# Decay logits and four keys' convolutions among the first products, and N stored whole, in a decoder step on one core

## The chip, the cores and the metric

The kernel runs on one core of a Trainium2 chip. Its engines are TensorE (PE), VectorE (DVE), ScalarE (ACT), GpSimd (POOL) and SyncE (SP). They run side by side and wait for each other through semaphores. SP and POOL issue most of the DMAs. The metric is the device time of one execution in microseconds, as the median of several runs. A profiled execution gives the trace.

## The reference, cut to what matters

One decoder layer for 512 prompt tokens and 8 sample tokens, D = 2048. A projection `w_in` gives q, k and v of 8 heads (128 wide), a gate z, a beta and a decay logit per head, and pool channels.

```python
qkv_c, new_conv = short_conv(conv_buf, qkv, conv_w)      # 4 taps along the tokens, then silu
q, k = l2norm(q) * (DN_HEAD_DIM ** -0.5), l2norm(k)
beta = jax.nn.sigmoid(b_raw)
g = -jnp.exp(a_log) * jax.nn.softplus(a_raw + dt_bias)
o, S = gated_delta_chunked(q, k, v, g, beta, S0)
dn_out = rmsnorm(o, dn_norm) * silu(z)
h = h + concat([dn_out, pool_out]) @ w_out
h = h + swiglu(rmsnorm(h, norm_ffn))
...
```

The gated delta rule needs, for each chunk of tokens, a triangular matrix N of k's inner products (weighted with beta and the decays), the inverse of 1 + N, here called U, and a state S that runs through the chunks.

## The kernel before

All activations lie transposed, channels on partitions and the 520 tokens (8 sample, 512 prompt) along the row. Each fp32 operand is split into a high and a low part, and a product takes three passes (high by high, low by high, high by low). ACT makes the high parts, DVE the low ones (`hi`, `lo`; `L294`/`L295` in pairs, `L135`/`L137` in plain products).

**Stages.** First x is turned and normed and the first two columns of `w_in` are multiplied (to some 48 us). Then come five pairs of columns: two plain ones (`Pair.plain`, called with `to_plain` and `to_strassen`) with tiles 10 to 13, which are keys 2 to 5, and three in Strassen's form (`strassen` with seven products of 24 matmuls each; the hook `after(q, j)` is called ahead of product j of pair q). In these two stages the order of every engine's instructions is the order of the program. From about 155 us on the woven stage follows: TensorE still goes in program order, the other engines in an order that a scheduler plans from priorities and estimated times; `tc.high_priority(offset=AHEAD)` lifts an instruction ahead of others. It computes the remaining columns with `product`, and between its steps `weave.step()` runs two tracks of generators: each `yield n` says that the next part comes n steps later. A tile of columns has 16 steps, and a step lies behind six matmuls. After the weave come `w_out` and the feed-forward part, up to the end at 2196 us, which the change doesn't touch.

**In the weave.** Track 0 starts with `states` (five pieces of sample states are transposed on TensorE at steps 11 to 15), later the recurrence `delta(h)`, one head after the other. Track 1 starts with `gates`: 64 products of `wba` with x for beta and decay logits (`L912`, `L913`), their transposes, some 35 small operations on DVE and ACT, and the sums of decays. Behind it come `keys(h)` for 8 heads: products of the convolved key with itself (`L1155`), its transposes (`L1158`), norms (ACT squares, POOL power), N (`L1170`) and kd (`L1172`); five steps later the diagonal 32 x 32 blocks of N are stored to `nd_d` and zeroed in N. N and k of heads 4 to 7 go to `kept_d`; all four share one place for N. Each `keys(h)` also convolves key h + 2 (`take_k`). `eliminate` loads the blocks (`nb`), inverts them in 31 steps of two DVE operations (`L1200`, `L1202`), stores U and its transpose to `ud_d`, loads them back as `utf` and adds `delta(0)` to the track, 60 steps later.

`delta(h)` first multiplies N by U (`L1234`), improves U in three iterations (`L1253`) and then goes through four chunks: R from S (`L1282`, `L1284`), W (`L1289`, ACT copy `L1291`), S (`L1294`, DVE `L1297` for the first chunk, `L1299` for others) and the output (`L1300`, `L1301`). `take_qv(h + 1)` convolves the next head's q and v in one go. A convolution (`convolved`) loads a column from `c_d`, and takes one DVE tensor-scalar (`L1097`), three taps of scalar-tensor-tensor (`L1099`) and a Silu on ACT (`L1100`).

PSUM has eight banks: three rotate as `mm` (products of the weave and of `product`), five as `dn` (all the rest). A tile takes the next bank in turn and waits until all reads of the bank's last tile are done.

## Time and profile before

| | |
|---|---|
| median of 3 runs | 2198.32 us (2196.6 to 2199.14) |
| the profiled execution | 2198.01 us |
| its span, first to last instruction | 2196.3 us |
| PE, DVE, ACT, POOL busy | 2139.0, 1786.2, 958.0, 455.7 us |
| mean granted TensorE clock | 0.994 |

A row of a view names the line of the kernel, the engine, the operation and its tiles as out<-in; times are microseconds from the start of the span. What stands in brackets behind a row is the engine's idle time before it and what ended it. Busy TensorE is not TensorE at its peak, since the ends of matmuls are modelled. A granted clock of 1.0 is 2.4 GHz, 0.5 is 1.2 GHz.

### The profile page before, as it was taken

The page shows a single profiled execution, that of the slowest core. Times are in us where ns is not written, and L with a number is a line of the kernel's source. Part 1 is how long each engine was busy: PE and PEld are TensorE (multiplying, and loading weights), DVE is VectorE, ACT ScalarE, POOL GpSimd, SP SyncE. Part 2 cuts the span into 40 slices and gives each one's busy share as a digit, 9 for nine tenths or more (in the row PEclk, how much of TensorE's full clock was granted, in tenths as well). Part 3 has the DMA queues.
Part 4 walks back from the last instruction along what each step waited for, and adds up shares of the span by engine and source line. Part 5 has one row for each costly group of instructions (what it writes and reads, how often), then busy time and mean ns, then how long its engine had stood idle before and what let it go on. Part 6 is the DMA issues. An engine that isn't in the chain of part 4 may idle for free.

```text
span 2196.3 us, 43075 instructions
## 1 busy us (share of the span) xinstructions
PE 2139.0 (97%) x17737; PEld 2127.6 (97%) x17737; DVE 1786.2 (81%) x2635; ACT 958.0 (44%) x1454; POOL 455.7 (21%) x559
## 2 busy tenths in 40 slices
PE   7999979999999999999999999999999999999998
PEld 7999979999999999999999999999999999999998
DVE  7788766665569979988888898888887798887997
ACT  6346513433335445343443443443433534435544
POOL 2112201110002210433323323323012402103100
PEclk9999989999999999999999999999999999999999
DMA  8444634432435552554555545445445836447333
GB/s 277 125 135 140 188 107 137 119 108 65 125 99 159 157 150 71 169 154 132 161 152 150 149 147 164 144 144 159 126 124 172 274 108 179 138 109 238 96 107 117
DMA packets 451553, 316.98 MB, mean 144 GB/s; under 512 B 27676, under 2 KB 424373, under 8 KB 448013
## 3 DMA queue, kind: packets, MB, share of 16 engines
q1 hardware_dynamic: 429741, 232.59, 37.5%
q0 software_dynamic: 20448, 80.91, 11.3%
q8 instruction: 139, 2.28, 0.4%
q10 hardware_dynamic: 1168, 0.74, 0.1%
q14 instruction: 57, 0.47, 0.1%
HBM read 261.97 MB, written 52.87 MB: 143 GB/s over the span
## 4 chain that ended last, share of the span: by engine, by line
PE 77%; DVE 11%; DMA 4%; ACT 3%; issue 3%; POOL 1%; SPq 0%; ACTq 0%; DVEq 0%; POOLq 0%
PE dn L301 21%; PE dn L302 21%; PE dn L303 21%; PE mm L170 3%; PE mm L172 3%; PE mm L171 3%; DVE lo L295 2%; DVE lo L137 1%; DMA vT<-c_d 1%; DVE y L1099 1%; ACT hi L294 1%; DVE raw L323 1%; DMA st<-a_d 1%; DMA raw<-in_w_in_dram 0%; DVE tm L1200 0%
## 5 line engine op out<-in xcount | busy, mean ns | idle before, releaser
L294 ACT CAST hi<-raw 128x1024 fp32r<-128x1024 f32 (+1 forms) x447 | 453.1, 1027 | 439.1 <-DVE raw L323 218.2
L295 DVE TENSOR_TENSOR lo<-raw,hi 128x1024 fp32r<-128x1024 f32 (+1 forms) x447 | 556.8, 1265 | 104.4 <-ACT hi L294 102.8
L170 PE MATMUL mm<-xh,hi 128*128 128x264 f32 (+1 forms) x960 | 291.1, 303 | 1.4 <-DVE ext L261 0.7
L171 PE MATMUL mm<-xl,hi 128*128 128x264 f32 (+1 forms) x960 | 272.5, 284 | 1.3 <-DVE xl L586 1.1
L172 PE MATMUL mm<-xh,lo 128*128 128x264 f32 (+1 forms) x960 | 272.6, 284 | 1.1 <-DVE lo L137 1.1
L170 PEld LDWEIGHTS mm<-xh,hi 128*128 128x128 f32 x960 | 182.7, 190 | 2.4 <-DVE ext L261 0.9
L171 PEld LDWEIGHTS mm<-xl,hi 128*128 128x128 f32 x960 | 183.0, 191 | 1.9 <-DVE xl L586 1.9
L172 PEld LDWEIGHTS mm<-xh,lo 128*128 128x128 f32 x960 | 181.9, 189 | 1.6 <-DVE lo L137 1.6
L323 DVE TENSOR_TENSOR raw<-raw 128x1024 f32<-128x1024 f32 (+1 forms) x136 | 180.5, 1327 | 2.3
L302 PE MATMUL dn<-b21l,hi 128*128 128x260 f32 x620 | 175.7, 283 | 0.1
L303 PE MATMUL dn<-b21h,lo 128*128 128x260 f32 x620 | 175.4, 283 | 0.0
L303 PE MATMUL dn<-b11h,lo 128*128 128x260 f32 x612 | 173.2, 283 | 1.8 <-DVE lo L295 1.8
L301 PE MATMUL dn<-b21h,hi 128*128 128x260 f32 x620 | 175.0, 282 | 0.0
L302 PE MATMUL dn<-b11l,hi 128*128 128x260 f32 x612 | 173.3, 283 | 0.0
L301 PE MATMUL dn<-b11h,hi 128*128 128x260 f32 x612 | 172.8, 282 | 0.0
L301 PE MATMUL dn<-T1h,hi 128*128 128x260 f32 x556 | 158.1, 284 | 0.0
L302 PE MATMUL dn<-T1l,hi 128*128 128x260 f32 x556 | 157.7, 284 | 0.0
L303 PE MATMUL dn<-T1h,lo 128*128 128x260 f32 x556 | 156.8, 282 | 0.0
L301 PE MATMUL dn<-B22h,hi 128*128 128x260 f32 x548 | 155.9, 284 | 0.0
L302 PE MATMUL dn<-B22l,hi 128*128 128x260 f32 x548 | 155.6, 284 | 0.0
L303 PE MATMUL dn<-B22h,lo 128*128 128x260 f32 x548 | 154.6, 282 | 0.4 <-DVE lo L295 0.4
L1605 POOL TENSOR_TENSOR mixa<-mixa 128x520 f32<-128x520 f32 x22 | 51.2, 2326 | 495.7 <-DVE mixa L1599 495.7
(729 smaller groups left out, 6923.2 us busy)
## 6 DMA issues: line engine op xcount, KB each, us to landing
raw<-in_w_gate_up_dram SPq DMA_DIRECT2D x134, 512.0 KB
raw<-in_w_in_dram SPq DMA_DIRECT2D x75, 512.0 KB
a_d<-mixa POOLq DMA_DIRECT2D x22, 1040.0 KB, 5.5
raw<-in_w_down_dram SPq DMA_DIRECT2D x48, 448.0 KB
mixb<-in_w_gate_up_dram SPq DMA_DIRECT2D x41, 512.0 KB
raw<-in_w_out_dram SPq DMA_DIRECT2D x25, 512.0 KB
st<-a_d POOLq DMA_DIRECT2D x49, 260.0 KB, 6.5
raw<-in_w_down_dram SPq DMA_DIRECT2D x24, 512.0 KB
```

The lines of the kernel that those rows point to most:

```text
L137: dve.tensor_tensor(lo[:, r], raw[:, r], hi[:, r].bitcast(F32), op=ALU.subtract)
L170: te.matmul(acc[ci], wh, hi[k][:, c0:c1], start=(i == 0), stop=False)
L171: te.matmul(acc[ci], wh, lo[k][:, c0:c1], start=False, stop=False)
L172: te.matmul(acc[ci], wl, hi[k][:, c0:c1], start=False, stop=(i == len(w) - 1))
L294: act.copy(hi, raw)
L295: dve.tensor_tensor(lo, raw, hi.bitcast(F32), op=ALU.subtract)
L301: te.matmul(acc, wh[:, k, :], xf[:, k, :], start=start and k == 0, stop=False)
L302: te.matmul(acc, wh[:, k, :], xg[:, k, :], start=False, stop=False)
L303: te.matmul(acc, wl[:, k, :], xf[:, k, :], start=False, stop=stop and k == wh.shape[1] - 1)
L323: dve.tensor_tensor(r[name], r[a], r[b], op=op)
L1099: dve.scalar_tensor_tensor(y, x[:, i:i + SEQ], cw(i, t), y, op0=ALU.mult, op1=ALU.add)
L1605: pool.tensor_tensor(q[:, 4:8:2, :], q[:, 1:4:2, :], q[:, 0:2, :], op=ALU.subtract)
```

## The change

The logits with all that follows from them (`gates`) become nine steps called from `to_plain` and `to_strassen`, with banks of the `mm` rotation and scratch in parts of `mixa`; the second half of the logit products stands ahead of the first pair, the first half in it. Their results move to another pool of tiles. Keys 2 to 5 are convolved between the Strassen products: loads at `after(0, 1)` and `after(1, 1)`, one operation per listed slot. In every convolution the load goes to POOL's queue, and the first tap from DVE to ACT. `keys` run in the order 2, 3, 0, 1, 4, 5, 6, 7, with 8 steps from one to the next up to the fifth and 11 from there on; only keys 0, 1 (ahead of the weave), 6 and 7 are convolved in the weave. N is stored whole to `nn_d` with one DMA on POOL, without zeroing; its blocks are loaded from there, those of heads 0 to 3 already after key 1. The blocks are zeroed later (`no_blocks`). `delta(0)` comes 58 instead of 60 steps after the elimination is issued. In `delta` the ten operations of the next q and v are spread, one per step, from the second iteration on; R, W and S get high priority.

```diff
+    def convolution(x, t, place):
+
+        ys = []
+
+        def load():
+            pool.memset(x[:, 0:3], 0.0)
+            pool.dma_start(x[:, 3:3 + SEQ], c_d[t])
+
+        def first():
+            ys.append(place())
+            act.activation(ys[0], x[:, 0:SEQ], AF.Copy, scale=cw(0, t))
+
+        def tap(i):
+            return lambda: dve.scalar_tensor_tensor(ys[0], x[:, i:i + SEQ], cw(i, t), ys[0], op0=ALU.mult, op1=ALU.add)
+
+        return [load, first, tap(1), tap(2), tap(3), lambda: act.activation(x[:, 3:3 + SEQ], ys[0], AF.Silu)]
...
             if i == 14:
+                split(wba[:, :, 0:16], wba[:, :, 16:32], wba_raw)
...
+        def row(k, a, b):
+            return mixa[:, k, HALF + a:HALF + b]
...
+        banks = {}
+
+        def bank(n):
+            banks[n] = ps_mm.tile([P, HALF], F32, tag="mm", name="mm")
+            return banks[n]
+
+        def logits(half):
+            pa, c = bank(f"a{half}")[:32, :], slice(HALF * half, HALF * half + HALF)
+            for k in range(KT):
+                te.matmul(pa, wba[:, k, :], xh[:, k, c], start=(k == 0), stop=False)
+                te.matmul(pa, wba[:, k, :], xl[:, k, c], start=False, stop=(k == KT - 1))
+
+        def logits_out(half):
+            c = slice(HALF * half, HALF * half + HALF)
+            dve.tensor_tensor(bas[:, c], banks[f"a{half}"][:32, :], rb[:32, c], op=ALU.mult)
...
+        def gates(step):
+            if step == 0:
+                logits(0)
+                logits_out(0)
+                act.activation(al, al, AF.Exp)
+            elif step == 1:
+                pt = bank("t")
+                for c in range(NCH):
+                    te.transpose(pt[:, 32 * c:32 * c + 32], bas[:, NB + P * c:NB + P * (c + 1)], ident[:32, :32])
+                te.transpose(pt[:NB, 128:160], bas[:, 0:NB], ident[:32, :32])
+            elif step == 2:
...
+                act.activation(u, ax, AF.Abs)
+                act.activation(u, u, AF.Exp, scale=-1.0)
+                act.activation(eb, eb, AF.Exp, scale=-1.0)
+            elif step == 3:
+                dve.tensor_scalar(s, u, 2.0, None, op0=ALU.add)
+                dve.reciprocal(s2, s)
...
+                dve.reciprocal(btok, eb)
+            elif step == 4:
+                pass
+            elif step == 5:
+                g4 = gtok[:, 0:4, :].rearrange("p c h -> p (c h)")
+                pg = bank("g")
+                te.matmul(pg[:, 0:32], triu, g4, start=True, stop=True)
+                te.matmul(pg[:, 32:64], stril, g4, start=True, stop=True)
+                te.matmul(pg[:, 64:96], ones, g4, start=True, stop=True)
+                for i in range(2):
+                    pr = bank(f"r{i}")
+                    for c in range(2):
+                        te.matmul(pr[:H, P * c:P * (c + 1)], gtok[:, 2 * i + c, :], triu, start=True, stop=True)
...
+            elif step == 6:
+                pg = banks["g"]
...
+            elif step == 8:
+                te.matmul(bank("e")[:, 0:128], ones[:NB, :], ds_.rearrange("p a b -> p (a b)"), start=True, stop=True)
+            else:
+                dve.tensor_copy(sgb.rearrange("p a h b -> p (a h b)"), banks["e"][:, 0:128])
         pairs = [InPair(14), InPair(24), InPair(26)]
+        logits(1)
         plain_pairs[0].cut("A12")
...
+        logits_out(1)
 
         def to_plain(step):
+            gates(step)
...
         def to_strassen(step):
+            gates(5 + step)
...
+        early = [convolution(places(h)[0], 8 + h, lambda k=k: mixa[:, 6 + k % 2, 0:SEQ]) for k, h in enumerate((2, 3, 4, 5))]
+        slots = [(0, 5), (0, 6), (1, 0), (1, 1), (1, 2), (1, 4), (1, 5), (1, 6), (2, 0), (2, 1), (2, 3), (2, 5), (2, 6)]
+
         def after(q, j):
 
+            if j == 1 and q < 2:
+                for c in early[2 * q:2 * q + 2]:
+                    c[0]()
+            if (q, j) == (0, 3):
+                early[0][1]()
+            if (q, j) in slots:
+                k, i = divmod(slots.index((q, j)), 3)
+                if i == 0 and k:
+                    early[k - 1][5]()
+                if k < 4:
+                    early[k][2 + i]()
+                if i == 1 and k < 3:
+                    early[k + 1][1]()
...
-        nd_d = dram.tile([H, 4, NCH, 32, 32], F32, name="nd_d")
-        ud_d = dram.tile([H, 4, 2, NCH, 32, 32], F32, name="ud_d")
+        nn_d = dram.tile([P, H * NCH, 4, 32], F32, name="nn_d")
+        ud_d = dram.tile([4, H, 2, NCH, 32, 32], F32, name="ud_d")
+        kept_d = dram.tile([4, 2, P, SEQ], F32, name="kept_d")
...
         def take_qv(h):
+
             x = [d1tile(tag, [P, 528], name)[:, 13:528] for tag, name in (("s0", "qT"), ("s2", "vT"))]
-            qvs[h] = convolved(x[0], h), convolved(x[1], 16 + h)
+            qvs[h] = [a[:, 3:3 + SEQ] for a in x]
+            q, v = (convolution(a, t, lambda: d1tile("y", [P, SEQ], "y")) for a, t in zip(x, (h, 16 + h)))
+            return [lambda: (q[0](), v[0]()), *q[1:5], lambda: (q[5](), v[1]()), *v[2:]]
...
+        def no_blocks(h):
+
+            nn3 = v3(mixb[:, 4 + h % 4, 0:SEQ])
+            for q in range(4):
+                r = slice(32 * q, 32 * q + 32)
+                pool.memset(nn3[r, :, r], 0.0)
...
-            if h + 2 < H:
-                take_k(h + 2)
+            if h in (0, 5):
+                take_k({0: 6, 5: 7}[h])
...
-            nn3 = v3(nn)
-            for q in range(4):
-                r = slice(32 * q, 32 * q + 32)
-                sp.dma_start(nd_d[h, q].rearrange("c s j -> s c j"), nn3[r, :, r])
-            for q in range(4):
-                r = slice(32 * q, 32 * q + 32)
-                pool.memset(nn3[r, :, r], 0.0)
+            pool.dma_start(nn_d[:, NCH * h:NCH * h + NCH], nn.rearrange("p (n r j) -> p n r j", n=NCH, r=4))
             if h >= 4:
-                for i, y in enumerate((kT, nn, kd)):
+                for i, y in enumerate((kT, kd)):
                     sp.dma_start(kept_d[h - 4, i], y)
             if h == H - 1:
                 weave.add(eliminate(), 1)
+            else:
+                if h == 1:
+                    nbs.append(d1tile("nb", [P, 32, 32], "nb"))
+                    blocks(0)
+                yield 3 if h < 4 else 6
+
+        nbs = []
+
+        def blocks(half):
+
+            for q in range(4):
+                p0 = 32 * q + 16 * half
+                pool.dma_start(nbs[0][p0:p0 + 16], nn_d.rearrange("(q s) n r j -> q r n s j", q=4)[q, q, 16 * half:16 * half + 16])
...
+            nb = nbs[0]
+            blocks(1)
+            for h in range(4):
+                no_blocks(h)
...
-            take_qv(0)
-            weave.add(delta(0), 0, 60)
+            for f in take_qv(0):
+                f()
+            weave.add(delta(0), 0, 58)
...
-            if h not in qvs:
-                while 16 + h not in traced:
-                    yield 1
-                take_qv(h)
-                yield 12
             qT, vT = qvs[h]
+            to_come = []
+
+            def more():
+                if to_come:
+                    to_come.pop(0)()
...
-                if it == 2 and 17 + h in traced:
-                    take_qv(h + 1)
+                    if h + 1 < H:
+                        assert 17 + h in traced
+                        to_come = take_qv(h + 1)
+                more()
...
+                    R = d1tile("R", [P, P], "R")
+                    with tc.high_priority(offset=AHEAD):
+                        dve.scalar_tensor_tensor(R, kp[:, 0:P], negc[:, c, h:h + 1], vs[:, ck(c)],
+                                                 op0=ALU.mult, op1=ALU.add)
+                    more()
...
-                act.copy(W, wp[:, 0:P])
+                with tc.high_priority(offset=AHEAD):
+                    act.copy(W, wp[:, 0:P])
+                more()
                 yield 2
...
+                with tc.high_priority(offset=AHEAD):
+                    if S is None:
+                        dve.tensor_copy(S2, dp[:, 0:P])
+                    else:
+                        dve.scalar_tensor_tensor(S2, S, egl[:, c, h:h + 1], dp[:, 0:P], op0=ALU.mult, op1=ALU.add)
...
+            if 0 < h < 5:
+                no_blocks(h + 3)
...
-        weave.add(gates(), 1)
-        for h in range(H):
+        for h in (2, 3, 0, 1, 4, 5, 6, 7):
             weave.add(keys(h), 1)
```

## Rows read from the trace of the kernel before

**Rows 1.** The page's first part: busy time, share of the span and instructions of each engine.

```profile
PE 2139.0 (97%) x17737; PEld 2127.6 (97%) x17737; DVE 1786.2 (81%) x2635; ACT 958.0 (44%) x1454; POOL 455.7 (21%) x559
```

**Rows 2.** Waits of TensorE in the window from 155 to 550 us: line, what it waited for: total, times, longest.

```profile
PE dn L1234 <- DMA utf<-ud_d: 13.6, 1, 13.6
PE dn L1282 <- DVE S L1297: 8.6, 6, 2.0
PE dn L1155 <- ACT mixa L1100: 4.3, 1, 4.3
PE dn L1158 <- DVE mixb L1170: 2.8, 1, 2.8
...
PE mm L170 <- DVE ext L261: 0.7, 1, 0.7
...
PE dn L1282 <- DVE S L1299: 0.4, 1, 0.4
```

**Rows 3.** Stretches of 10 us: width, PE busy (x matmuls), PE weight loads, DVE, ACT, POOL busy, then the granted clock, the DMAs' share and GB/s.

```profile
230.00:240.00 10.00, 5.27 (x27) 5.07 (x28) 8.59 (x22) 4.95 (x12) 3.20 (x8) 0.71 0.78 243
240.00:250.00 10.00, 10.00 (x82) 10.00 (x82) 8.76 (x26) 5.30 (x10) 2.52 (x7) 0.95 0.36 113
...
300.00:310.00 10.00, 2.30 (x11) 2.33 (x12) 0.71 (x1) 0.27 (x1) 0.61 (x1) 0.50 0.44 132
310.00:320.00 10.00, 10.00 (x83) 10.00 (x82) 5.07 (x13) 2.73 (x10) 2.63 (x6) 0.87 0.40 100
320.00:330.00 10.00, 8.22 (x56) 8.02 (x56) 5.41 (x9) 3.49 (x5) 0.00 (x0) 0.83 0.36 109
```

**Rows 4.** Timelines of TensorE, DVE and SP, in order of time, from the last key's products to the recurrence's first: start, duration, engine, line, operation.

```profile
236.07 2.08 PE L1155 MATMUL dn<-mixa 128*128 128x128 f32 x8 [4.35 <-ACT mixa L1100]
...
260.80 0.34 DVE L1170 SCALAR_TENSOR_TENSOR mixa<-dn,sck,dm 128x128 f32<-128x128 f32 x1
...
266.88 0.34 SPq L1190 DMA_DIRECT2D nb<-nd_d  x1
...
271.19 0.21 DVE L1200 TENSOR_TENSOR tm<-nb,u 128x31 f32<-128x31 f32 x1 [1.23 <-DMA nb<-nd_d]
...
299.45 0.19 DVE L1202 TENSOR_TENSOR u<-u,tm 128x31 f32<-128x31 f32 x1
...
304.75 5.32 SPq L1127 DMA_DIRECT2D utf<-ud_d  x9
...
307.70 1.14 PE L1234 MATMUL dn<-utf,mixb 128*128 128x96 f32 x4 [13.63 <-DMA utf<-ud_d]
```

**Rows 5.** The logit products by line: count, duration in ns (min/median/max), first and last start, forms.

```profile
L912 PE MATMUL dn<-xh,wba x32: 276/280/288, 158.3 to 167.8; 128*32 128x264 f32 x16, 128*32 128x256 f32 x16
```

**Rows 6.** Longer stretches, columns as in rows 3: the first two Strassen pairs, and the woven products behind the last key.

```profile
92.00:112.00 20.00, 20.00 (x169) 20.00 (x169) 17.73 (x25) 7.53 (x8) 4.80 (x8) 1.00 0.45 132
112.00:132.00 20.00, 20.00 (x169) 20.00 (x168) 16.52 (x21) 8.08 (x9) 4.22 (x6) 1.00 0.61 176
...
241.00:294.00 53.00, 53.00 (x441) 52.77 (x440) 43.90 (x106) 22.52 (x24) 7.74 (x25) 1.00 0.52 148
```

**Rows 7.** Instructions of a convolution by line: tensor-scalar tap, scalar-tensor-tensor taps, Silu; count, duration in ns (min/median/max), first and last start.

```profile
L1097 DVE TENSOR_SCALAR y<-mixb,prm x4: 467/488/1898, 160.5 to 180.8; 128x512 f32<-128x512 f32 x4
...
L1099 DVE SCALAR_TENSOR_TENSOR y<-mixb,prm,y x12: 730/747/753, 162.4 to 184.3; 128x512 f32<-128x512 f32 x12
...
L1100 ACT ACTIVATE mixb<-y x4: 632/632/634, 167.0 to 185.1; 128x512 f32<-128x512 f32 x4
```

**Rows 8.** Timelines of DVE and TensorE: a low part in the third Strassen pair and the first matmul that uses it.

```profile
143.17 1.22 DVE L295 TENSOR_TENSOR lo<-raw,hi 128x1024 fp32r<-128x1024 f32 x1
...
148.99 0.29 PE L303 MATMUL dn<-xh,lo 128*128 128x260 f32 x1
```

**Rows 9.** Timelines of TensorE and DVE: key 1's products at 198.05 and its N at 210.25, key 3's products at 207.55 and the wait of its transposes at 211.43.

```profile
198.05 1.05 PE L1155 MATMUL dn<-mixb 128*128 128x128 f32 x8
...
207.55 1.05 PE L1155 MATMUL dn<-mixb 128*128 128x128 f32 x8
...
210.25 1.12 DVE L1170 SCALAR_TENSOR_TENSOR mixb<-dn,sck,dm 128x128 f32<-128x128 f32 x4
...
211.43 0.66 PE L1158 MATMUL dn<-ident,mixb 128*128 128x128 f32 x4 [2.83 <-DVE mixb L1170]
```

**Rows 10.** Stores of convolution inputs by line, 256 KB each, issued on POOL: duration of the issue in ns, and time to landing in us.

```profile
L476 POOL DMA_DIRECT2D c_d<-ext x24: 539/547/700, 46.3 to 479.0; - x24
...
DMA to landing us min/median/max: 2.3/2.5/6.7
```

**Rows 11.** Timeline of DVE in the second head's first chunk.

```profile
354.11 1.22 DVE L137 TENSOR_TENSOR lo<-raw,hi 128x1024 fp32r<-128x1024 f32 x1
355.24 0.75 DVE L1099 SCALAR_TENSOR_TENSOR y<-vT,prm,y 128x512 f32<-128x512 f32 x1
355.90 0.28 DVE L1297 COPY S<-dn 128x128 f32<-128x128 f32 x1
```

**Rows 12.** Waits of POOL in the window from 155 to 550 us, columns as in rows 2.

```profile
POOL ccs L474 <- DVE ext L261: 93.1, 14, 15.5
```

**Rows 13.** Timeline of POOL at the start of the woven stage.

```profile
160.29 1.85 POOL L1068 MEMSET utf<- 128x1024 f32 x2 [17.97 <-DVE mixa L502]
```

180 lines of the change are left out of this document (64 added, 116 removed).

## The prediction

> **What bounds the kernel.** The first line of the page puts TensorE at 97% of the span [rows 1], so a part of the change is worth what it does to TensorE's remaining idle time and to its clock, and work of other engines costs nothing unless TensorE waits for it. The second view is therefore the list of TensorE's waits from 155 to 550 us, the stretch that the change rewrites [rows 2]: 13.6 us before the first product of the recurrence (`L1234`), for U's blocks to come back from DRAM; 8.6 and 0.4 us at `L1282` for the state S; 4.3 us at `L1155` for a convolved key; 2.8 us at `L1158`, for a PSUM bank that the N of an earlier key still holds; 0.7 us for an eviction. Together 30.4 us. The third view is the granted clock in 10 us windows [rows 3]. It falls to its lower level, 1.2 instead of 2.4 GHz, after the two long waits. A mean of 0.71 in 230 to 240 us is 5.8 us at the lower level; TensorE idles until 236.07 [rows 4], so 3.9 us are worked at half speed, which loses 2.0; 240 to 250 loses 0.5; from 307.70 on 1.15, 1.3 (0.87) and 1.7 (0.83). Together 6.6 us. So at most 30.4 + 6.6 = 37.0 us can be had in this stretch.
>
> **Moved TensorE work.** The 64 logit products (0.28 us each as a record [rows 5], one started every 0.12 us, as 441 in 53.0 us show [rows 6]) and the few small ones behind them take some 9 us wherever they stand. Cost and gain 0, if the pairs don't make them wait. Their 35 or so small DVE and ACT operations go with them, into a stretch that is lengthened by those same 9 us.
>
> **Convolutions in the pairs.** Twelve taps of 0.75 us [rows 7] enter DVE's fixed order: two in the first pair, six in the second, four in the third. DVE is busy 17.73 and 16.52 of 20 us in the first two [rows 6]; with 1.5 and 4.5 us they hold 19.2 and 21.0, so the second overruns by 1 us. What stands behind a tap on DVE is the next low part, and for that TensorE waits. Its margin is 4.6 us (ready at 144.39, used at 148.99 [rows 8]). Below: 0. Above: had they no cover at all, 9.0 us. I take 0.5, since 1 us is far inside the margin. One Silu (0.63 us [rows 7]) stands on ACT in front of the first weights of the woven stage, for which TensorE already waits there: 0.6. The cover of the loads is two blocks of products between issue and first use.
>
> **Weave steps.** A step carries six products, 0.72 us [rows 6]. Counting the yields, the logits held the keys' track until step 31, and the keys then ran every 5 steps, the last at 66. Now the keys start at step 1, every 8 and later 11 steps, and the last is again at 66. The first recurrence comes at step 139 instead of 141. The end of the weave is thus unmoved, the keys have twice the time, and four convolutions and all decay logits have gone from DVE.
>
> **The wait for U.** Before, the last key was multiplied at 236.07, its N was complete only at 261.14, its blocks landed for 271.19, the elimination ran to 299.64, and U was back for 307.70 [rows 4]. Of the first 25.1 us most is queue: the N of keys 4 to 7 share one place, with four small stores, four memsets and a whole store between two of them. Key 1 needed 13.3 us from 198.05 to 211.37, behind other keys' work [rows 9]; I take 11.5 for the lighter queue. Then one whole store of N through POOL, 0.55 issue and 2.5 landing [rows 10]; four block loads, 2.2 and 2.5; the elimination 28.45 and the way out and back 8.05 as before [rows 4]. Sum 55.75 us. TensorE arrives after its own 1.5 and 73 steps, 54.1 us. Remaining wait 1.65, taken as 2. Bounds: 0, and the old 13.6 with the 4.15 us of clock behind it.
>
> The keys' waits of 4.3 and 2.8 fall away with the early convolutions and the wider spacing. What is late next is a **bank**. Five PSUM banks rotate among keys (two each) and the five pieces of the sample states. Formerly the logits kept the keys away from those pieces; now keys stand at steps 1 and 9 and the pieces at 11 to 15, so the fourth piece takes a bank that key 3 must release, and products queue behind it in TensorE's fixed order. From that key's first product to the piece are 1.5 + 5 x 0.72 + 1.5 = 6.6 us. If its N takes 13.3 us [rows 9], TensorE waits 6.7; if it keeps 6.6, nothing. I take 3.5, in the middle, and 1.0 for clock lost to such a wait.
>
> **The recurrence.** In the second head a low part of 1.22 us and a tap of 0.75 us ran ahead of the copy of S [rows 11]. With one tap a step, S, R and W first in priority and the first tap on ACT, the tap goes, the low part stays. Of 8.6 + 0.4 us I leave 3; bounds 0 and 9.0. POOL gains some 41 DMA issues of 0.55 us [rows 10], about 22 us; behind the keys it is busy 7.74 of 53 us [rows 6], and SP loses as many. On POOL they stand behind copies that wait for evictions [rows 12].
>
> The longest POOL issue of a convolution input is 0.70 us against a median of 0.547 [rows 10], so DVE hardly holds up POOL's DMAs. One tensor-scalar tap took 1.898 us against 0.488 [rows 7] while POOL ran two memsets at 160.29 [rows 13]. The Trainium skill (SBUF — State Buffer, "SBUF: two separate sides") warns against just this move: descriptors of a DMA issued on POOL are written by GpSimd, which a two-port DVE operation locks out of the shared port, so such DMAs belong on SP or ACT. The stretched tap agrees with a shared port, the issue times show no starving. By the rule each DMA would wait for at most one such operation, 0.49 us, and the two in U's chain would leave the wait at 3 instead of 2.
>
> **Sum.** The profiled execution took 2198.01 us, the median of the runs is 0.3 above. Removed 37.0; new or left 0.5 + 0.6 + 2 + 3.5 + 1.0 + 3 = 10.6; gain 26.4. 2198.3 - 26.4 = 2172.
>
> **Rivals.**
> *U is still late*: the chain is bound by something else than the queue, say DVE, or POOL's issue. The elimination and U's way back, 36.5 us of it, are unchanged [rows 4]. Against it: the 25.1 us before N. With 13.6 + 4.15 instead of 2: 2188.
> *The bank wait is long*: 6.7 us, the clock loss of 2.5 seen after 4.35 us of idling [rows 3, 4], and one further wait like the 2.8 [rows 2], 12 instead of 3.5: 2180. For it: the order of the five pieces; against: DVE has lost the four taps of each early key.
> *Slower, by POOL's queue*: a q or v load stands behind a copy that waits for an eviction. Such waits lasted 93.1 us over 14, 6.7 each [rows 12]. The first tap on ACT then waits 6.7 + 2.5 = 9.2, and W behind it, whose slack is two steps, 1.4 us: 7.8 us in each of seven heads, 54: 2226. It decides from 5.2 us of lateness on (26.4 / 7 + 1.4). Against: the order on POOL, ACT and DVE is planned, and the loads have two steps of lead.
> *Nothing gained*: U's wait stays whole and the pairs lose 7.5 of the taps' 9.0 us: 2195.
>
> **Numbers.** Forecast (2161 to 2178) 0.57; U late (2182 to 2192) 0.14; bank (2178 to 2184) 0.12; nothing gained 0.06; slower 0.11. A measurement of this kernel can't tell less than 0.2%, 4.4 us, from no change. Faster 0.83, same 0.06, slower 0.11. The low end is all 37 us gone, 2161; the high end takes in the bank case and most of the late U: 2161 to 2190. The forecast's own range is 2161 to 2178.
>
> **What would show it.** Right: the wait at the first product of the recurrence under 4 us and no lower clock behind it; no wait for the convolved key; S waits under 4 us in all; the pairs still without idle time on TensorE; the logit products between 45 and 75 us. Wrong: a wait on the states' transposes or a key's over 7 us, low parts late in the second pair, or ACT waiting in each head for a load.

## The result and the profile after

The change made the kernel slower: 2209.11 us (2204.74 to 2210.76, median of 5) against 2196.6 us, a ratio of 1.005 (95% interval 1.0034 to 1.0065), where 2172 us had been forecast. The profiled execution took 2204.74 us, its span 2203.0, 6.7 more than the span before; TensorE works as long as before [rows 1], and waits more. The profiled execution is the fastest of the five and had the highest clock, 0.995 in the mean against 0.991 to 0.993, so what follows accounts for these 6.7 us and not for the whole distance of the medians, 12.5.

The first part of the page, and the granted clock in the stretches around the longest waits (columns as in rows 3 and 6):

```profile
PE 2138.5 (97%) x17737; PEld 2124.9 (96%) x17737; DVE 1773.2 (80%) x2612; ACT 960.2 (44%) x1470; POOL 479.6 (22%) x600
```

```profile
170.00:180.00 10.00, 7.07 (x44) 6.65 (x44) 7.83 (x18) 7.13 (x15) 1.71 (x2) 0.83 0.48 141
220.00:230.00 10.00, 6.64 (x57) 6.43 (x56) 7.49 (x19) 5.85 (x7) 3.21 (x7) 1.00 0.84 242
...
300.00:310.00 10.00, 0.00 (x0) 0.00 (x0) 4.46 (x14) 0.00 (x0) 0.00 (x0) 0.60 0.43 150
310.00:320.00 10.00, 8.48 (x61) 8.52 (x62) 2.96 (x11) 1.95 (x9) 3.15 (x7) 0.72 0.26 41
...
132.00:152.00 20.00, 18.55 (x153) 18.12 (x152) 14.75 (x22) 7.27 (x11) 1.17 (x2) 1.00 0.59 176
```

TensorE's waits from 155 to 550 us, the answer to [rows 2]:

```profile
PE dn L1304 <- DMA utf<-ud_d: 14.6, 1, 14.6
PE dn L1369 <- ACT W L1365: 5.2, 6, 1.5
PE mm L170 <- DVE ext L261: 3.4, 1, 3.4
PE dn L1354 <- DVE S L1373: 3.3, 5, 1.0
...
PE dn L1083 <- DVE mixb L1230: 1.5, 1, 1.5
...
```

The wait for U is whole (`L1304` is the old `L1234`). The waits for a convolved key are gone; two pieces of the sample states (`L1083`) and an eviction (`L261`) wait in their place. Of the 9.0 us of waits for S 5.5 went, and 5.2 came for W. The pairs, which had no idle time, have some.

Timelines of TensorE, DVE, POOL and SP from the last key's products to the first product with U, the answer to [rows 4]:

```profile
242.69 1.05 PE L1215 MATMUL dn<-mixa 128*128 128x128 f32 x8
...
257.74 1.12 DVE L1230 SCALAR_TENSOR_TENSOR mixa<-dn,sck,dm 128x128 f32<-128x128 f32 x4
...
259.15 0.54 POOL L1234 DMA_DIRECT2D nn_d<-mixa  x1 [3.51 <-DVE mixa L1230]
264.11 1.30 POOL L1252 DMA_DIRECT2D nb<-nn_d  x2 [4.41 <-DMA nn_d<-mixa]
266.05 0.25 POOL L477 COPY ccs<-ext 128x8 f32<-128x8 f32 x1 [0.64 <-DVE ext L261]
...
267.45 1.27 POOL L1252 DMA_DIRECT2D nb<-nn_d  x2
...
275.06 0.43 DVE L261 TENSOR_TENSOR ext<-mm,rb 128x264 f32<-128x264 f32 x1 [1.09 <-PE mm L172]
275.41 0.20 DVE L1269 TENSOR_TENSOR tm<-nb,u 128x31 f32<-128x31 f32 x1
...
303.65 0.19 DVE L1271 TENSOR_TENSOR u<-u,tm 128x31 f32<-128x31 f32 x1
...
308.36 3.80 SPq L1187 DMA_DIRECT2D utf<-ud_d  x8
...
311.52 1.78 PE L1304 MATMUL dn<-utf,mixb 128*128 128x96 f32 x7 [14.63 <-DMA utf<-ud_d]
```

A table of all kernels stands ahead of the experiments, since they are read by it. It is worked out from the timeline of TensorE in the one profiled execution of each kernel, while the ratios come from all executions: "idle" is the sum of the stretches without a matmul, up to the last matmul and by stretch (the hole is that in front of the first product with U, in 240 to 320 us with a little else), and "clock" is half of the time worked at 1.2 GHz. Idle and clock together account for the difference of each span from that of before to within some 4 us: after and before differ by 4.0 of 6.7 us, the last kernel and before by 15.6 of 15.5. The clock's loss is also a matter of the execution: the five of the changed kernel, with the same instructions, were granted 0.991 to 0.995.

| kernel | ratio to before (95%) | idle | clock | 90-180 | 180-240 | 240-320 | 320-560 | 560-700 |
|---|---|---|---|---|---|---|---|---|
| before | 1 | 51.0 | 6.6 | 1.5 | 8.3 | 13.6 | 10.1 | 4.1 |
| after | 1.005 (1.0034-1.0065) | 57.8 | 3.8 | 7.6 | 6.0 | 14.6 | 9.9 | 5.4 |
| n_on_sp | 1.0043 (1.0031-1.0055) | 53.8 | 4.2 | 6.5 | 6.6 | 14.5 | 7.5 | 5.9 |
| blocks_out | 1.0016 (1.0007-1.0025) | 47.5 | 6.6 | 7.2 | 4.7 | 8.3 | 9.1 | 5.4 |
| key7_first | 1.0036 (1.0018-1.0053) | 48.4 | 10.7 | 6.3 | 6.0 | 7.0 | 9.7 | 5.0 |
| keys_as_before | 1.0026 (1.0016-1.0035) | 54.1 | 6.2 | 10.2 | 7.3 | 8.1 | 8.6 | 5.0 |
| keys_later | 1.0018 (1.0009-1.0026) | 48.8 | 11.6 | 4.3 | 9.5 | 8.7 | 10.1 | 2.4 |
| first_on_dve | 1.0085 (1.0071-1.0098) | 58.8 | 12.6 | 7.0 | 7.5 | 13.1 | 11.7 | 5.0 |
| recurrence_as_before | 1.0099 (1.0085-1.0113) | 62.2 | 13.5 | 7.4 | 8.0 | 13.8 | 14.6 | 3.7 |
| loads_on_sp | 0.9991 (0.9983-1.0) | 43.1 | 6.4 | 6.9 | 6.1 | 6.4 | 5.4 | 5.3 |
| qv_on_sp | 1.004 (1.0027-1.0053) | 53.4 | 10.3 | 7.2 | 5.9 | 15.6 | 5.7 | 5.8 |
| late20 | 1.0015 (1.0007-1.0023) | 51.2 | 10.7 | 7.6 | 7.9 | 3.0 | 12.6 | 6.0 |
| before_late20 | 0.9965 (0.9952-0.9978) | 38.9 | 9.8 | 1.2 | 7.6 | 4.8 | 4.8 | 7.4 |
| before_late10 | 1.0 (0.9991-1.0008) | 46.6 | 8.1 | 1.2 | 6.5 | 8.3 | 4.7 | 10.3 |
| combined | 1.0038 (1.0026-1.005) | 49.6 | 8.8 | 2.3 | 5.0 | 14.8 | 10.9 | 2.5 |
| sp_blocks | 1.001 (1.0001-1.0019) | 47.6 | 6.9 | 6.3 | 7.2 | 9.4 | 5.9 | 5.1 |
| sp_keys_later | 1.0018 (1.0009-1.0027) | 50.2 | 11.1 | 4.3 | 8.7 | 8.6 | 11.8 | 2.5 |
| sp_late8 | 0.9972 (0.9963-0.9981) | 43.7 | 8.5 | 7.4 | 7.4 | 1.0 | 6.5 | 8.4 |
| best | 0.9947 (0.9934-0.9961) | 38.6 | 3.4 | 6.7 | 5.6 | 1.4 | 5.9 | 5.1 |

### The profile page after: what moved, and what is told of

Read it like the earlier page. It is cut to its first block, busy times and chain, and to the rows that moved or that the text cites. A ratio compares the mean times of both kernels' runs of the same rounds, so it can differ in the third digit from the quotient of the medians.

```text
span 2203.0 us, 43043 instructions
## 1 busy us (share of the span) xinstructions
PE 2138.5 (97%) x17737; PEld 2124.9 (96%) x17737; DVE 1773.2 (80%) x2612; ACT 960.2 (44%) x1470; POOL 479.6 (22%) x600
## 3 DMA queue, kind: packets, MB, share of 16 engines
q0 software_dynamic: 23296, 89.84, 12.6%
## 4 chain that ended last, share of the span: by engine, by line
PE 78%; DVE 10%; DMA 4%; ACT 3%; issue 2%; POOL 1%; ACTq 0%; SPq 0%; DVEq 0%; POOLq 0%
PE dn L301 21%; PE dn L302 21%; PE dn L303 21%; PE mm L170 3%; PE mm L172 3%; PE mm L171 3%; DVE lo L295 2%; DMA vT<-c_d 1%; DVE y L494 1%; ACT hi L294 1%; DVE lo L137 1%; DMA st<-a_d 1%; DVE raw L323 1%; PE dn L1323 0%; DMA mixa<-c_d 0%
```

## The experiments

"Key to N" counts here, as in the expectations, from the second half of key 7's products to the end of its N.

### U's chain: queue, form of the transfers, or key 7

**n_on_sp.**

```diff
-            pool.dma_start(nn_d[:, NCH * h:NCH * h + NCH], nn...)
+            sp.dma_start(nn_d[:, NCH * h:NCH * h + NCH], nn...)
-                pool.dma_start(nbs[0][p0:p0 + 16], nn_d...)
+                sp.dma_start(nbs[0][p0:p0 + 16], nn_d...)
```

> The changed kernel with two issues moved back to SP's queue: the whole store of N and the eight loads of its blocks. Everything else on POOL stays there. Theory A (POOL's queue makes U late: the block loads stand behind copies that wait for evictions, and behind the store's landing): from the end of key 7's N to the first step of the elimination the time falls from 17.7 us (258.86 to 275.41, and 1.1 more on DVE) to about 9, the hole of 14.6 us to 6, and the kernel gains 7 to 10 us: 2200. Theory B (it is the form of the transfers, pieces of 128 bytes on the way in where they were on the way out before, and the wait for two landings in a row): the time from N to the elimination stays within 2 us of 16.5, the hole at 13 to 16, and the kernel is the same within 2 us. Theory C (SP's queue holds them up behind the loads of weights that wait for a free buffer): the hole grows by 3 us or more.

From N's end to the elimination 19.7 us instead of 16.55; the hole is 12.75 all the same, since N was ready 4.8 us sooner behind its key. A is out, and neither B (within 2 us of 16.5) nor C (a longer hole) holds as it was put: on SP loads of weights stand between the block loads, and on DVE the elimination stands behind a low part that waited 5.61 us for its high part. The ratio can't be told from that of the changed kernel. So SP's queue was no better for these transfers; what POOL's costs them is not shown by it.

**blocks_out.**

```diff
-            pool.dma_start(nn_d[:, NCH * h:NCH * h + NCH], nn...)
+            for q in range(4):
+                r = slice(32 * q, 32 * q + 32)
+                pool.dma_start(nd_d[q, h].rearrange("c s j -> s c j"), v3(nn)[r, :, r])
...
-            blocks(1)
+            pool.dma_start(nb.rearrange("p s j -> p (s j)"), nd_d.rearrange("q h c s j -> (q h c) (s j)"))
```

> The changed kernel with N's four diagonal blocks cut out on the way to DRAM again, as four stores behind each key, and one load of all blocks of whole rows of 4 KB ahead of the elimination, all still issued on POOL; the whole N goes out too, on SP, for keys 4 to 7 only. Theory A (storing N whole put the cutting into pieces of 128 bytes behind the last key instead of behind each, and that, not the queue, made U late): from the end of key 7's N to the elimination the time falls from 16.55 us to 10 or 11 (10.04 before), the hole from 14.6 to 8 or 9, the kernel gains 5 to 7 us. Theory B (POOL's queue, where the issues stand behind copies that wait for evictions): it stays above 15 us, and the kernel is the same or, with 24 more issues of 0.55 us on POOL, slower.

POOL's timeline and the first step of the elimination on DVE, then TensorE's waits from 240 to 320 us:

```profile
255.63 2.23 POOL L1237 DMA_DIRECT2D nd_d<-mixa  x4 [3.46 <-DVE mixa L1231]
...
263.08 0.57 POOL L1258 DMA_DIRECT2D nb<-nd_d  x1 [5.02 <-DMA nd_d<-mixa]
...
267.31 0.21 DVE L1270 TENSOR_TENSOR tm<-nb,u 128x31 f32<-128x31 f32 x1 [3.58 <-DMA nb<-nd_d]
```

```profile
PE mm L170 <- DVE ext L261: 8.0, 3, 6.2
...
```

12.0 us instead of 16.55, and TensorE no longer waits for U: near A's numbers, still on POOL's queue, and 7 us faster than the changed kernel by the two ratios. A's reason is shown for 1 us only. Here DVE takes the blocks as they land. In the changed kernel the last block load, issued at 268.08, landed 3.8 us later, at 271.8, 13.0 us behind N's end; DVE's order then had a low part and an eviction in front of the first step, at 275.41 (the load's own view, then DVE's timeline):

```profile
DMA to landing us min/median/max: 3.8/3.8/3.8
...
272.74 1.23 DVE L137 TENSOR_TENSOR lo<-raw,hi 128x1024 fp32r<-128x1024 f32 x1 [3.63 <-ACT hi L135]
```

So of the 4.6 us that blocks_out takes off this stretch, 1.0 is the transfers' (13.0 against 12.0) and 3.6 the place of the elimination in DVE's order; key to N was 5.2 us shorter as well (10.6 against 15.7), by no edit of its own. And a new wait of 6.2 us stands at 269 us, which is the price of that place: DVE's order has the elimination in front of an eviction, so DVE first waits 3.58 us for the blocks and then runs ten steps and a low part, until 274.98, before it evicts the bank.

**key7_first.**

```diff
+            with tc.high_priority(offset=AHEAD) if h == H - 1 else ExitStack():
                 _, dm = decay(h)
                 ...
                 dve.tensor_tensor(v3(kd), v3(ktp), bc3(ad), op=ALU.mult)
```

> The changed kernel with the decay mask, squares, norms, N and kd of key 7 alone put ahead of other work in the planned order of DVE, ACT and POOL (as the copies of S, R and W are). TensorE's order is untouched. Theory A (N is late because the queue of ACT, with a Silu and its table loads between the squares, and POOL's small copies stand in front of key 7): from key 7's first product to the end of its N the time falls from 15.7 us to 9 or less, the hole from 14.6 us to 7 or 8, the kernel gains 6 to 8 us. Theory B (the way from N to the elimination, 16.55 us against 10.04 before, takes it back, since it ends at work that other engines order): the N is earlier by 6 us, the elimination by less than 2, and the hole stays above 12.

Key to N 8.2 us instead of 15.7, the hole 6.97: A for the chain, not for the time. The ratio is 0.14% lower, which the intervals do not tell from nothing; in the two profiled executions the idle time fell by 9.4 us and the clock's loss rose by 6.9, behind waits that were hardly longer.

### The convolutions in the pairs

**keys_as_before.**

```diff
-        early = [convolution(places(h)[0], 8 + h, ...) for k, h in enumerate((2, 3, 4, 5))]
-        ... (their loads, taps and Silus between the products)
-            if h in (0, 5):
-                take_k({0: 6, 5: 7}[h])
+            if h + 2 < H:
+                take_k(h + 2)
-        for h in (2, 3, 0, 1, 4, 5, 6, 7):
+        for h in range(H):
```

> The changed kernel without the convolutions of keys 2 to 5 in the first pairs: they are done again when the key two places earlier is multiplied, and the keys go in the order 0 to 7. The decay logits stay between the pairs, N is stored whole, the queues and the recurrence are as changed. Theory A (the twelve taps, four first taps and Silus cost the pairs TensorE's time on the fixed order of DVE and ACT): TensorE's gaps of 0.3 us and more between 120 and 172 us, 5.7 us in the changed kernel, fall to under 2 us (the kernel before had 0.7 in the same place), the first product of the woven stage comes 4 us earlier; what the keys then lose stands against it, the wait for a convolved key of up to 4 us, so 2205 to 2212 in all. Theory B (it is the logits' 35 small operations, the loads of other weights or the later start that make the low parts late): the gaps stay at 5 us or more, and the first product of the woven stage moves by less than 1.5 us.

The pairs' gaps behind the logits are gone, and TensorE waits instead for key 0, which now stands at step 1 (waits from 120 to 240 us):

```profile
PE dn L1199 <- ACT mixb L496: 7.8, 1, 7.8
PE mm L170 <- DVE ext L261: 3.5, 2, 2.3
...
```

So the taps did cost the pairs some 5 us (A). Although the keys take that back, it is 0.24% faster; what is shorter is the hole (6.8 us), since key 7's N took 8.5 us.

**keys_later.** As keys_as_before, and

```diff
-            weave.add(keys(h), 1)
+            weave.add(keys(h), 1, 0 if h else 16)
...
-                yield 3 if h < 4 else 6
+                yield 2
```

> The changed kernel without the convolutions in the pairs, as keys_as_before, but with the keys put at steps 16, 23, 30 and so on to 65 of the woven stage, behind the pieces of the sample states, where keys_as_before has them at steps 1, 9, 17 and so on to 66. Theory A (with the keys as late as before and 7 steps apart, nothing waits for a convolved key, and the banks are free): the wait of 7.82 us for key 0 and the 3.8 us of waits of the states' transposes go, the pairs stay free (gaps under 1.5 us in all), and the kernel is 6 to 9 us faster than keys_as_before, 12 faster than the changed kernel: 2193 to 2195. Theory B (every key has its wait wherever it stands): new waits for a convolved key or an eviction of 5 us or more between 175 and 245 us, and no gain on keys_as_before.

Mostly B: the 7.8 us went, 5.9 us for a transposed key and 3.6 us for an eviction came, and 11.6 us were lost to the clock; 0.08% faster than keys_as_before, inside both intervals.

### The recurrence

**first_on_dve.**

```diff
-            act.activation(ys[0], x[:, 0:SEQ], AF.Copy, scale=cw(0, t))
+            dve.tensor_scalar(ys[0], x[:, 0:SEQ], cw(0, t), None, op0=ALU.mult)
```

> The changed kernel with the first tap of the convolutions of the woven stage on DVE (a product with a scalar, 0.49 us) instead of on ACT (0.71 us). The four keys convolved in the pairs keep theirs on ACT. Theory A (in the recurrence ACT's first tap waits for its load, 26.0 us over 6, at most 6.9, and holds up the copy of W behind it): the waits of TensorE for W, 5.2 us over 6, fall under 2; those for S rise by no more than 1; the kernel gains 3 to 4 us. Theory B (the lateness goes to DVE, which now waits for the same loads): W's waits fall and S's and R's rise by as much, the kernel is the same within 2 us.

W's waits fell from 5.2 to 1.5 us and S's rose from 3.5 to 8.7: B, and worse, 0.35% slower than the changed kernel, with 8.8 us more lost to the lower clock.

**recurrence_as_before.** The same, and

```diff
-                        to_come = take_qv(h + 1)
-                more()
+                if it == 2 and h + 1 < H:
+                    for f in take_qv(h + 1):
+                        f()
...
-                with tc.high_priority(offset=AHEAD):
+                if True:
```

> The changed kernel with the recurrence's part undone: the q and v of the next head are convolved in one go behind the third iteration, the first tap on DVE in the whole woven stage, R, W and S without priority. Theory A (spreading the taps gave nothing: 8.6 us of waits for S and W before, 8.6 after, another engine in front): TensorE's idle time from 320 to 560 us stays at 9 to 11 us and the kernel is the same within 2 us. Theory B (the priority and the spreading are worth what was forecast, and only the ACT tap spoils it): the waits for S come back at 9 us while those for W go, the same sum, but first_on_dve is then better than both by 3 us. Theory C (spreading costs): it is faster by 3 us or more.

None of the three: 0.49% slower than the changed kernel, S's waits 11.5 us and W's 1.4. Spreading, priority and ACT's tap together do pay. By first_on_dve 0.35 of the 0.49% are ACT's tap; the 0.14% left for spreading and priority lie inside the intervals, with S's waits 2.8 us shorter. The forecast's waits for S were right, and W's are the part that spoiled them.

### The queue of the convolutions' loads

**loads_on_sp.**

```diff
-            pool.dma_start(x[:, 3:3 + SEQ], c_d[t])
+            (queue or pool).dma_start(x[:, 3:3 + SEQ], c_d[t])
...
-            for f in convolution(x, t, lambda: d1tile("y", [P, SEQ], "y")):
+            for f in convolution(x, t, lambda: d1tile("y", [P, SEQ], "y"), sp):
```

(and the same in `take_qv`; the four in the pairs stay on POOL)

> The changed kernel with the loads of the convolutions' inputs in the woven stage back on SP's queue; the stores of c_d, N and its blocks stay on POOL. Theory A (POOL's queue makes ACT's first tap late, 26.0 us of waits over 6 heads: the loads stand behind copies that wait for evictions): ACT's waits for them fall under 10 us, TensorE's for W, 5.2 us, under 2, and the kernel gains 3 to 5 us. Theory B (the load is late because it is asked for late, one step after its tile comes free): ACT's waits stay above 20 us and the kernel is the same within 2 us. Theory C (SP holds them up behind loads of weights): waits for W of 8 us or more, slower by 3 us or more.

0.59%, 13 us, faster than the changed kernel, three times A's gain, but not by A's way: ACT's waits for the loads fell from 26.0 to 17.9 us only, W's from 5.2 to 3.1, S's from 3.5 to 1.2, and most of the idle time that went is the hole's. Head 2's v in the changed kernel (timelines of TensorE, POOL and ACT), then the same in loads_on_sp:

```profile
350.10 0.60 PE L1338 MATMUL dn<-ident,vT 128*128 128x128 f32 x4
...
349.65 1.03 POOL L217 TENSOR_TENSOR fq<-ss,mhalf 128x4 f32<-128x4 f32 x1 [0.32 <-DVE ss L1314]
350.82 0.10 POOL L486 MEMSET vT<- 128x3 f32 x1
351.28 0.61 POOL L487 DMA_DIRECT2D vT<-c_d  x1 [0.35 <-issue]
...
355.88 0.72 ACT L491 ACTIVATE y<-vT,prm 128x512 f32<-128x512 f32 x1 [6.53 <-DMA vT<-c_d]
356.51 0.24 ACT L1365 COPY W<-dn 128x128 f32<-128x128 f32 x1
...
356.81 0.49 PE L1369 MATMUL dn<-W,kd 128*128 128x128 f32 x2 [1.52 <-ACT W L1365]
```

```profile
342.04 0.61 PE L1338 MATMUL dn<-ident,vT 128*128 128x128 f32 x4
...
342.72 0.33 SPq L487 DMA_DIRECT2D vT<-c_d  x1
...
346.86 0.72 ACT L491 ACTIVATE y<-vT,prm 128x512 f32<-128x512 f32 x1 [5.55 <-DMA vT<-c_d]
347.49 0.25 ACT L1365 COPY W<-dn 128x128 f32<-128x128 f32 x1
...
347.79 0.49 PE L1369 MATMUL dn<-W,kd 128*128 128x128 f32 x2 [0.55 <-ACT W L1365]
```

v's place comes free with its transposes, at 350.70 and 342.65. On POOL the load is issued 0.58 us later, behind a memset of the same place (the power ended at 350.68, just before the place was free), and has landed after 4.60; on SP 0.07 and 4.14. The difference, 0.97 us, is TensorE's: 1.52 against 0.55. In both, W stands on ACT behind a tap that waits for a load. The hole fell to 6.4 because key 7's N took 7.5 instead of 15.7 us; the loads around it were no longer in POOL's order, and the planned order of ACT and DVE around key 7 came out another.

**qv_on_sp.**

```diff
-            q, v = (convolution(a, t, lambda: ...) for ...)
+            q, v = (convolution(a, t, lambda: ..., sp if h else None) for ...)
```

> The changed kernel with only the loads of q and v for heads 1 to 7 on SP's queue, the ones inside the recurrence; the loads of keys and of head 0's q and v stay on POOL. loads_on_sp, with all of them on SP, gained 13 us: its hole was 6.4 instead of 14.6 us and its idle time in the recurrence 5.4 instead of 9.9. Theory A (two separate effects of POOL's queue: in the recurrence each load stands behind the power of the norms and the other load, 2 us; near key 7 the load and what is ordered around it delay N): here the recurrence falls to 5 or 6 us, the hole stays at 13 to 16, and the gain is 4 to 6 us. Theory B (it is the hole alone, a matter of key 7's order, that pays): the recurrence stays above 8 us and nothing is gained.

A for the waits: 5.7 us in the recurrence, the hole 14.6. Of the 4.2 us nothing can be seen in the time (1.004 against 1.005), against A; in the profiled executions 6.5 us more were lost to the clock. So 4.5 us of loads_on_sp's idle time are the recurrence's loads, and 8.2 the order around key 7; whether POOL's issue itself or only the order planned for it made key 7 late stays open.

### The place of the first recurrence

**late20 and before_late20.** In both, the last sample rows enter the operand of the output product after it was cut, so the output lacks them; the instructions are all there.

```diff
-            weave.add(delta(0), 0, 58)
+            weave.add(delta(0), 0, 78)
```

(60 and 80 in the kernel before)

> The changed kernel, with one number altered: the first recurrence is put 78 instead of 58 steps behind the start of the elimination, so its first product stands 20 steps of six products (14.4 us) later in TensorE's order. Nothing else is touched. Theory A (the 14.6 us hole is a matter of where the product stands in TensorE's order; U's chain of 68.7 us is as long as before): the wait at the first recurrence's product falls from 14.63 to under 1.5 us, the 4 us of products worked at the lower clock behind it come back too (2 us), and the kernel gains 14 to 17 us: 2192 to 2195 against 2209. Theory B (the hole is given back later: the recurrences, the sample states and the last pool products then stand closer to the end of the woven stage and wait for buffers and for each other): the hole goes, but new waits of 8 us or more stand between 560 and 680 us, and the gain is under 7 us.

> The kernel before, with the same one number altered: the first recurrence 80 instead of 60 steps behind the start of the elimination. Theory A: its hole of 13.63 us and the 4.15 us of products at the lower clock behind it go: 2197 - 17 = 2180, so that one number alone does most of what the whole change could. Theory B (given back later): 2190 or more. If both this kernel and the one above gain alike, the hole is independent of the change's other parts and those parts by themselves cost the difference that is left between the two (about 12 us).

The holes fell to 2.96 and 4.68 us, the gains are 0.35% each, about 7.7 us, in both between what A and B gave. In late20 the idle time fell by 6.6 us and the clock's loss rose by 6.9: the recurrence's waits for W rose from 5.2 to 6.9 us and for S from 3.5 to 4.8. Before, only the sample states paid, with 7.0 us at their end. The hole is a matter of order in both, and the two kernels stay 0.5% apart.

**before_late10.** 70 instead of 60.

> The kernel before with the first recurrence 70 instead of 60 steps behind the start of the elimination, so that its first product stands 10 steps, 7.2 us, later. From before_late20, where the wait for U fell from 13.63 to 4.68 us but 7.0 us appeared at the sums of the sample states' products at the end of the stage: the hole should be 6 to 9 us, the clock behind it still low for 4 us, and the wait at the sample states under 1 us, so 5 to 7 us faster than before: 2190. If it is no faster than before, the gain of before_late20 came from the order that the later place gave to DVE and ACT in the recurrence (4.8 us idle there instead of 10.1), not from the hole.

No gain: the hole was 7.75 us, the recurrence had 4.7 us of idle time, and 6.4 us stood at the output product. Hole and end together are 14.2 us, as much as the hole before, against 11.7 in before_late20. The recurrence's idle time fell here as it did there, so that order alone does not explain before_late20's gain either.

### Edits together

**combined** (keys_later, key7_first, blocks_out, and the product of step 8 of the gates one step later).

> The changed kernel with four of the single edits together: no convolutions in the pairs and the keys at steps 16 to 65 (keys_later), key 7's chain ahead in the planned order (key7_first), N's blocks cut on the way out (blocks_out), and the product of the gates' 128 columns one step later between the pairs. Theory A (they answer different waits and add up: pairs 5 to 6 us, U's chain 8.2 + 12 + 28.3 + 7.7 = 56 us against an arrival of 54, so a hole of 2, the bank 1.1): 2187 to 2190 against 2209 and 2196.6, better than both. Theory B (waits of 2 to 4 us scatter anew and each costs the clock behind it as well): the idle time falls by 15 us, but the time only to 2194 to 2198.

**sp_blocks** (loads_on_sp, blocks_out, the same shift of the gates) and **sp_keys_later** (loads_on_sp and keys_later).

> loads_on_sp together with blocks_out, and the product of the gates' 128 columns one step later between the pairs. Theory A (load queue and form of N's transfers are separate terms of U's chain): key to N 7.5, N to elimination 12, elimination 28.4, way out and back 8 us, 56 in all, so the hole falls from 6.4 to 2 or 3 us, the bank's 1.1 go too, and the kernel is 4 to 6 us faster than loads_on_sp: 2187. Theory B (the planned order of DVE shifts the wait, as in blocks_out, to an eviction of 6 us in front of the elimination, or to key 7's squares, as in the combined kernel): the wait of TensorE between 240 and 310 us stays above 6 us in sum, and nothing is gained on loads_on_sp.

> loads_on_sp together with keys_later: no convolutions in the pairs, the keys at steps 16 to 65. Theory A (the taps' loss in the pairs, 5.9 us of gaps, is a term of its own): the gaps between 120 and 172 us are under 1.5 us, the waits at the start of the woven stage no longer than in loads_on_sp, 3 to 6 us faster than loads_on_sp. Theory B (what the pairs give, the keys take: waits for a convolved key of 5 us or more, 5.9 us in keys_later): the same within 2 us or slower.

B in kind each time, though combined is outside both ranges (the idle time fell by 8.2 us, the time to 2204). In combined the waits for evictions (`L261`) between 175 and 320 us sum to 11.1 us over 6, key 7's N took 15.2 us in spite of its priority, and the hole was 8.8; in sp_blocks an eviction of 6.25 us at 270 took the hole's place; in sp_keys_later the 5.85 us for a transposed key came back. Here single gains did not add up.

**sp_late8** (loads_on_sp, and 66 instead of 58) and **best**, which also has

```diff
-                for task in (conv_out(), sample_norms(), *map(sample_product, range(H)), sample_out()):
+                for task in (sample_norms(), *map(sample_product, range(H)), sample_out(), conv_out()):
...
-            yield 8
+            yield 6
...
-                    yield 1
+                    if h >= 4 or b < 7:
+                        yield 1
...
-            gates(5 + step)
+            if step != 3:
+                gates(min(5 + step, 8))
```

> loads_on_sp with the first recurrence 66 instead of 58 steps behind the start of the elimination: 8 steps, 5.8 us, which is the most of its remaining hole of 6.4 us. Theory A: the hole is under 1.5 us, the 2.9 us lost at the lower clock behind it come back, the sample states still end 7 steps ahead of the output product: 5 to 8 us faster than loads_on_sp, 2185 to 2188. Theory B (as in late20: the later place gives as much back in short waits for W and S and the clock behind them): within 2 us of loads_on_sp.

> sp_late8 with the sample states made 8 steps shorter (the rows of the convolution's states go out behind them, the first sums wait 6 instead of 8 steps, four of the eight products take 7 instead of 8), so that they end where they did in the changed kernel, and the product of the gates' 128 columns one step later between the pairs. Theory A (the wait of 4.15 and 1.82 us that sp_late8 has at the output product stands for the last rows of the sample states and for nothing else): it falls to under 1.5 us, the 1.09 us at the bank go, and the kernel is 4 to 6 us faster than sp_late8: 2184 to 2186, 0.5% faster than the kernel before. Theory B (the loads of the sample states can't come faster): new waits for them of 4 us or more, and the same time as sp_late8.

sp_late8 is faster than both kernels (0.9972), though less than A said: the hole is 0.98 us, but the output product waits for the last sample rows:

```profile
PE mm L1628 <- ACT xh L196: 4.2, 1, 4.2
PE mm L1629 <- DVE xl L197: 1.8, 1, 1.8
```

best takes these away (A): 2183.21 us, 0.9947 (0.9934 to 0.9961). The later place and the shorter sample states were not tried together in the kernel before, where the place alone gave 0.35%, so what the rewrite itself adds to best stays open. Of its waits from 240 to 700 us:

```profile
PE dn L1357 <- DVE S L1376: 2.9, 5, 1.0
PE mm L1633 <- DVE xl L197: 2.0, 2, 1.1
...
PE dn L1307 <- DMA utf<-ud_d: 1.4, 1, 1.4
```

## Why the prediction was wrong

It was wrong in sign. Between 2172 and the profiled execution's 2204.7 lie 32.7 us (the median lies 4.4 higher); by the table 12.6 are U's, 5.8 the recurrence's, 5.0 the pairs', 2.0 the keys', 1.4 the sample states' and what follows, 2.8 the clock's; 3.1 I can't place.

**U.** The step that failed most. Its terms and what they measured: key to N, from the first product, 11.5, 16.2; store 3.05, 5.25 (259 to 264.11); blocks 4.7, 11.3; elimination 28.45, 28.4; out and back 8.05, 7.7; TensorE's arrival 54.1, 54.2. The sum is 68.8 instead of 55.75, so the rival "U is still late" took place, with three causes. The store and the load were priced by a whole store of 256 KB [rows 10], while the new loads take N apart in pieces of 128 bytes; these loads landed (issue to landing, eight of them, in the changed kernel) after

```profile
DMA to landing us min/median/max: 3.5/4.2/5.7
```

in two pairs, with copies between them. Of the 11.3 us "blocks", 7.7 are these loads; the other 3.6 are DVE's order, a term that the prediction did not have: the first step stood behind a low part and an eviction (blocks_out, above). How much of the store and the loads is the form in pieces is not settled: blocks_out, with N taken apart behind each key again, was 1.0 us shorter there, and the kernel before, on SP's queue, needed 10.0 us from N to the elimination, where these take 12.0 and 13.0 to the landing. And key to N was no queue for N's place: between key 7's squares, from 244.84 to 251.72 us, ACT's order has a Silu of v, two table loads of 1.28 us, key 7's own exponent and a high part, and up to N, at 257.74, DVE's has two low parts, two evictions and three taps of q; key7_first got it to 8.2 us, counted from the second half of the products. Over the kernels made from the changed one it came out between 7.5 and 16.9, though only key7_first and combined gave key 7 priority: it hangs on the planned order, which every edit changes.

The Trainium skill (DMA: Bandwidth & Descriptors, "Anatomy of one DMA — SWDGE (gpsimd) path") fits a DMA issued on GpSimd by 2.0 us and its bytes at 436 GB/s, an estimated 2.15 us for one of these 64-KB loads. The trace does not agree: 3.5 to 5.7 us, among other transfers.

**The pairs.** The cost was read from DVE's margin [rows 6, 8] and taken as 0.5 + 0.6. They lost 6.1: 1.1 at the bank of the gates' last product, 3.5 between the pairs' products, and 1.5 more at the woven stage's first weights (2.2 against 0.7). TensorE's waits from 90 to 175 us:

```profile
PE dn L303 <- DVE lo L295: 2.8, 5, 0.7
PE mm L170 <- ACT hi L135: 2.2, 1, 2.2
PE mm L929 <- DVE mixa L925: 1.1, 1, 1.1
...
PE dn L301 <- ACT hi L294: 0.7, 1, 0.7
```

The margin was spent by ACT, which I had counted only at its end. Timelines of ACT, DVE and TensorE:

```profile
136.29 0.72 ACT L491 ACTIVATE mixa<-mixa,prm 128x512 f32<-128x512 f32 x1 [3.43 <-DMA mixa<-c_d]
136.91 1.04 ACT L294 CAST hi<-raw 128x1024 fp32r<-128x1024 f32 x1
...
137.98 1.23 DVE L295 TENSOR_TENSOR lo<-raw,hi 128x1024 fp32r<-128x1024 f32 x1 [2.67 <-ACT hi L294]
...
142.22 0.42 ACT L530 ACTIVATE mixa<-mixa 128x260 f32<-128x260 f32 x1 [4.27 <-DVE mixa L528]
142.54 1.98 ACT L294 CAST hi<-raw 128x1024 fp32r<-128x1024 f32 x2
...
143.62 0.39 PE L301 MATMUL dn<-xh,hi 128*128 128x260 f32 x1 [0.71 <-ACT hi L294]
```

A first tap waits for its load, the high part behind it is late, DVE waits for that and is late with the output, whose Silu stands in front of the next high part. "The cover of the loads is two blocks of products" was wrong: key 4, whose tap this is, is loaded at `after(1, 1)` and first used at `after(1, 2)`, so it has one block, 24 matmuls or 2.9 us at 0.12 us each, for a load that was issued at 131.14 and used at 136.29.

**The recurrence.** S 3.3 + 0.2 us, near the 3 taken. What was missing is W, 5.2 us. The second half of the rival by POOL's queue was seen: the tap waits for the load, W for the tap. Its cause and its size were not: ACT waited 6.9 us at worst, not 9.2, for the landing and v's one place rather than for a copy's wait, and TensorE lost at most 1.5 us a head. With the loads on SP, W still cost 3.1 us.

**Right were** the logits (47.8 to 61.1 us), the keys' waits that go, the arrival of TensorE, and the bank as the next thing late: 2.6 us at the states' transposes instead of 3.5 (the profile names N's operation for 1.5 of them), and an eviction of 3.4 beside it. The clock lost 3.8, not 1.0.

The Trainium skill (SBUF — State Buffer, "SBUF: two separate sides") advises SP or ACT for such DMAs, and with the loads on SP the kernel was faster (0.9991 against 1.005). The reason it gives is not what the trace shows: POOL's issues of these loads took 0.54 to 0.62 us, within the 0.54 to 0.70 of its stores before [rows 10]; in six heads 0.3 to 1.9 us passed from v's place coming free to the issue, and 3.0 to 5.9 from there to the landing. Most of the gain came with the order around key 7.

## What to carry to other kernels

Where one engine's order is fixed, first ask whether the waiting product can stand later: eight steps in one number, with the work behind it shortened as much, took 0.44% off loads_on_sp, where the rewritten chain had left U as late as before. Price a chain by what the next engine still has in front of it when the last transfer has landed, and on every in-order engine name the instruction behind one that waits for a DMA. Gains found one at a time need not add up when a planner orders the other engines anew after each edit.

## What the runs showed of the hardware that was not expected

The clock's answer to a wait of 2 to 4 us is not the same each time. In qv_on_sp TensorE waited 3.94 us until 229.28 for the eviction for which it had waited 3.36 us in the changed kernel, whose clock stayed at 1.00 in 220 to 230 (above) and in the next 10 us. In qv_on_sp the next 10 us were worked at 0.73, so at 1.2 GHz for half the time:

```profile
230.00:240.00 10.00, 10.00 (x66) 10.00 (x65) 5.68 (x14) 6.04 (x17) 4.33 (x10) 0.73 0.69 200
```

In late20 the clock fell behind a wait of 1.89 us for S, with one of 0.87 just ahead (460 to 475 us):

```profile
460.00:475.00 15.00, 12.24 (x79) 11.84 (x78) 8.77 (x14) 4.88 (x8) 1.31 (x5) 0.77 0.30 91
```

Over the kernels the loss runs from 3.4 to 13.5 us in the one profiled execution of each, as much as the edits were worth, and in those of key7_first, qv_on_sp and late20 it ate most of what was gained in idle time or more. Whether the edit or the execution decides is not shown: the five executions of the changed kernel differ as well (0.991 to 0.995 in the mean).
